# A gather of rows by index: other places for the distinct indices, own loads for the first two batches, four direct batches instead of five

## The chip, the cores and the metric

The kernel runs on one core of a Trainium2 chip. The metric is the device time of one execution in microseconds (us), as the median over several runs. The profile also gives a span, from the first to the last recorded event; it is about 2 us shorter than the device time. A run on a single core is called slow here when it took over 1.5% more than the fastest run of the same kernel; comparisons use the fast runs alone.

## The reference

```python
x       = randn(32, 512, 1024)        # float32
indices = randint(0, 512, (32, 128))  # the same draw in every run
for b in range(32):
    result[b] = x[b, indices[b]]      # 128 rows of 4096 bytes
```

Some indices of a batch repeat: the draw has 109 to 120 distinct ones among the 128 of each batch.

## The kernel before

The first five batches (`HEAD`) are "direct": all 128 rows are gathered and written out. For each of the other 27 batches the kernel works out the distinct indices and gathers each distinct row only once. The remaining places, 8 to 18 in these batches, get an index out of bounds, and nothing is moved for them. A matmul with a matrix of zeros and ones then spreads the rows to their final places. These batches gather into a ring of eight buffers, which are zeroed first so that skipped places hold no leftovers.

```python
HEAD, RING, FAR = 5, 8, 1024
...
idx0 = const.tile([N, 1], indices.dtype, name="idx0")       # the indices of batch 0 by themselves
nc.sync.dma_start(out=idx0[:], in_=indices.rearrange("b n -> n b")[:, 0:1])
...
for b in range(HEAD):                                       # the direct batches
    gather(blocks[b], idx0[:].bitcast(I32)[:, 0:1] if b == 0 else idxT[:, b:b + 1], b)
    nc.sync.dma_start(out=of[b * N:(b + 1) * N], in_=blocks[b][:])
...
def prep(g0, g1):                                           # the "index step" of a group of batches
    ...                                                     # lead: first of its kind; slot: its rank
    for b in range(g0, g1):
        first = (79 * b) % N
        pack = junkp.tile([N, N], F16, name="pack")
        turned = turn[:].rearrange("p t n -> p (t n)")[:, N - first:2 * N - first]
        nc.vector.tensor_scalar(out=pack[:], in0=turned, scalar1=slot[:, b:b + 1],
                                scalar2=lead[:, b:b + 1], op0=ALU.is_equal, op1=ALU.mult)
        nc.tensor.matmul(sm[:, 1, b - g0:b - g0 + 1], lhsT=pack[:], rhs=near[:, b:b + 1], ...)
    nc.vector.tensor_scalar(out=at[:, w], in0=sm[:, 1, :n], ...)   # at: the indices to gather
...
for k in range(RING):                                       # eight zeroed buffers
    if k < 3:
        nc.vector.memset(u[:], 0.0)
    else:
        nc.scalar.copy(out=u[:], in_=held[0][:])            # five copies that read buffer 0
...
groups = [(HEAD, HEAD + 3)] + [(g, min(g + 4, B)) for g in range(HEAD + 3, B, 4)]
for b in range(HEAD, B):
    ...                                                     # prep of a later group
    u = held[(b - HEAD) % RING]
    gather(u, at[:, b:b + 1], b, bounds_check=S - 1, oob_is_err=False)
    ...                                                     # matmul, two copies out, write
```

The row `turned` says which place of the buffer each rank gets. Before, rank s of batch b goes to place (s + 79b) mod 128: the skipped places are one stretch, which moves on from batch to batch.

## Time and profile before

| | before |
|---|---|
| time, median of the first three runs | 89.34 us (88.88 to 89.35) |
| span of the profiled run | 87.1 us |
| moved | 32.12 MB |
| rate from 17 us to the last slice but two | about 418 GB/s |
| last packet of each of the 16 DMA engines | 82.5 to 85.5 us |

The prediction below shows the strips of this page and reads them. The busy time by stretches at the end (start and end, length, then busy us with counts for PE, its weight loads, DVE, ACT and POOL, then the clock, the DMA share and GB/s):

```profile
75.00:81.00 6.00, 3.85 (x8) 1.35 (x8) 1.75 (x3) 1.76 (x3) 0.00 (x0) 1.00 1.03 420
81.00:87.10 6.10, 0.00 (x0) 0.00 (x0) 0.00 (x0) 0.00 (x0) 0.00 (x0) 0.59 0.52 214
```

The rate stays at 420 GB/s to 81 us, when PE has been done for a while. The timeline near 20 us (start, duration, engine, line, operation, and in brackets the idle time before and what ended it):

```profile
17.40 0.99 POOL L79 DMA_INDIRECT u<-in_x_dram,at  x1 [0.30 <-issue]
20.34 0.35 PE L119 MATMUL sm<-near,pack 128*128 128x1 f16 x3 [4.06 <-DVE pack L117]
20.55 2.06 PE L148 MATMUL ps<-u,s 128*128 128x512 f32 x2
22.65 0.16 DVE L121 TENSOR_SCALAR at<-sm 128x4 int32<-128x4 f32 x1 [1.41 <-PE sm L119]
23.08 0.99 POOL L79 DMA_INDIRECT u<-in_x_dram,at  x1 [4.70 <-DVE atF L122]
```

Twelve gathers have been issued by 18.4 us. The thirteenth is the first of the third group and waits for that group's indices (`at`), which come at 22.65.

### The profile page before, as it was taken

To read this page: it belongs to the slowest core of one execution; us is meant where nothing else is said; L and a number is where in the kernel's file an instruction comes from. 1 tells how busy PE (TensorE), PEld (TensorE's weight loads), DVE (VectorE), ACT (ScalarE), POOL (GpSimd) and SP (SyncE) were. 2 spreads that over 40 slices of the span, in tenths; PEclk is the share of its full clock that TensorE was granted. 3 is DMA by queue.
4 is the path that set the end of the run, shared out by engine and by line. 5 is a ranking of instruction groups with operands and counts; after the bars stand their busy time and mean duration, and the time that the engine had idled before them with its cause. 6 is when DMAs were issued, how large, how long until landed. Compare 5 with 4: busy or idle time off the path is not lost.

```text
span 87.1 us, 784 instructions
## 1 busy us (share of the span) xinstructions
PE 58.0 (67%) x169; PEld 23.9 (27%) x169; DVE 47.3 (54%) x181; ACT 21.9 (25%) x33; POOL 32.3 (37%) x38
## 2 busy tenths in 40 slices
PE   0043502006999999999999999877978877793000
PEld 0031301003434444433443443222322333230000
DVE  4989994107539979587997357833141133333000
ACT  0997000000022222342322234031222222223000
POOL 3577787740354464618545461663200000000000
PEclk9999999999999999999999999999999999999855
DMA  0178999999999999999999999999999999999960
GB/s 4 27 207 224 322 373 363 416 421 418 418 420 420 416 421 418 420 416 421 418 421 410 416 420 427 406 420 420 418 420 418 420 420 414 421 420 420 414 256 15
DMA packets 9603, 32.12 MB, mean 369 GB/s; under 512 B 1751, under 2 KB 1783, under 8 KB 9600
## 3 DMA queue, kind: packets, MB, share of 16 engines
q1 hardware_dynamic: 4848, 16.80, 47.3%
q0 software_dynamic: 4608, 15.24, 45.5%
q10 hardware_dynamic: 144, 0.05, 0.2%
q8 instruction: 1, 0.02, 0.1%
q14 instruction: 2, 0.02, 0.0%
HBM read 16.84 MB, written 16.78 MB: 386 GB/s over the span
## 4 chain that ended last, share of the span: by engine, by line
DMA 35%; DVE 19%; issue 13%; PE 12%; POOL 7%; another core or an unknown queue 3%; ACT 1%; POOLq 1%; DVEq 0%
DMA u<-in_x_dram,at 35%; PE ps L148 11%; POOL u L79 7%; DVE junk L105 6%; DVE pack L117 4%; DVE u L133 2%; DVE block L150 2%; DVE s L125 2%; ACT block L151 1%; POOLq L79 1%; PE bc L101 1%; DVE slot L112 0%; DVE lead L108 0%; PE sm L119 0%
## 5 line engine op out<-in xcount | busy, mean ns | idle before, releaser
L148 PE MATMUL ps<-u,s 128*128 128x512 f32 x108 | 53.2, 629 | 4.5 <-DMA u<-in_x_dram,at 4.2
L79 POOL DMA_INDIRECT u<-in_x_dram,at x27 | 26.7, 990 | 25.5 <-DVE atF L122 9.1
L150 DVE COPY block<-ps 128x512 f32<-128x512 f32 x27 | 18.6, 691 | 22.9 <-PE ps L148 19.1
L151 ACT COPY block<-ps 128x512 f32<-128x512 f32 x27 | 15.8, 586 | 56.3 <-DVE block L150 54.1
L148 PEld LDWEIGHTS ps<-u,s 128*128 128x128 f32 x108 | 19.0, 196 | 29.4 <-issue 27.2
L105 DVE SCALAR_TENSOR_TENSOR junk<-bc,idxF,below 128x128 f16<-128x128 f32 x27 | 8.8, 345 | 0.9 <-issue 0.5
L117 DVE TENSOR_SCALAR pack<-turn,slot,lead 128x128 f16<-128x128 int32 x27 | 7.6, 358 | 2.9 <-remote 2.8
L101 PE MATMUL bc<-vf,ident 32*128 32x128 f16 x27 | 3.3, 263 | 7.7 <-DVE ident L67 5.0
L125 DVE TENSOR_SCALAR s<-bc,atF 128x128 f32<-128x128 f32 x27 | 7.6, 345 | 0.1
L119 PE MATMUL sm<-near,pack 128*128 128x1 f16 x27 | 3.4, 174 | 5.2 <-DVE pack L117 5.0
L119 PEld LDWEIGHTS <-pack 128*128 128x128 f16 x27 | 2.5, 102 | 11.4 <-DVE pack L117 8.2
L101 PEld LDWEIGHTS <-ident 32*128 32x128 f16 x27 | 2.1, 113 | 9.8 <-DVE ident L67 5.0
L135 ACT COPY u<-u 128x1024 f32<-128x1024 f32 x5 | 4.8, 1041 | 0.0
L79 POOL DMA_INDIRECT block<-in_x_dram,idxT x4 | 3.8, 941 | 1.5 <-issue 0.9
L111 PE MATMUL sm<-lead,above 128*128 128x4 f16 (+1 forms) x7 | 1.2, 170 | 3.7 <-DVE junk L105 2.3
L133 DVE MEMSET u<- 128x1024 f32 x3 | 2.7, 912 | 1.3 <-PEq L167 1.0
L121 DVE TENSOR_SCALAR at<-sm 128x4 int32<-128x4 f32 (+1 forms) x7 | 1.1, 162 | 2.5 <-PE sm L119 2.3
L105 DVE DVE_READ_ACCUMULATOR junk<-bc,idxF,below 128x1 f32 x27 | 2.3, 84 | 0.0
L135 ACT ACT_TABLE_LOAD x1 | 1.3, 1283 | 2.1 <-issue 2.1
L111 PEld LDWEIGHTS <-above 128*128 128x128 f16 x7 | 0.7, 103 | 3.7 <-DVE junk L105 2.6
L112 DVE COPY slot<-sm 128x4 f32<-128x4 f32 (+1 forms) x7 | 1.1, 155 | 1.2 <-issue 1.2
L79 POOL DMA_INDIRECT block<-in_x_dram,idx x1 | 1.1, 1098 | 1.6 <-DMA idx<-in_indices_dram 1.6
(17 smaller groups left out, 5.9 us busy)
## 6 DMA issues: line engine op xcount, KB each, us to landing
out_dram<-block SPq DMA_DIRECT2D x32, 512.0 KB, 8.9
u<-in_x_dram,at POOLq DMA_INDIRECT x27
block<-in_x_dram,idxT POOLq DMA_INDIRECT x4
v<-in_indices_dram ACTq DMA_DIRECT2D x2, 8.0 KB
v<-in_indices_dram SPq DMA_DIRECT2D x2, 8.0 KB, 1.8
v<-in_indices_dram ACTq DMA_DIRECT2D x1, 32.0 KB
idx<-in_indices_dram SPq DMA_DIRECT2D x1, 1.0 KB
block<-in_x_dram,idx POOLq DMA_INDIRECT x1
```

The lines of the kernel that those rows point to most:

```text
L79: nc.gpsimd.indirect_dma_start(out=dst[:], out_offset=None, in_=xf[:], in_offset=bass.IndirectOffsetOnAxis(ap=at, axis=0), element_offset= ...
L101: nc.tensor.matmul(bc[:, b - g0], lhsT=ident[:B, b:b + 1].to_broadcast([B, N]), rhs=vf[:], start=True, stop=True)
L105: nc.vector.scalar_tensor_tensor(out=junk[:], in0=bc[:, b - g0], scalar=idxF[:, b:b + 1], in1=below[:], op0=ALU.is_equal, op1=ALU.mult, ac ...
L111: nc.tensor.matmul(sm[:, 0, :n], lhsT=above[:], rhs=lead16[:, w], start=True, stop=True)
L117: nc.vector.tensor_scalar(out=pack[:], in0=turned, scalar1=slot[:, b:b + 1], scalar2=lead[:, b:b + 1], op0=ALU.is_equal, op1=ALU.mult)
L119: nc.tensor.matmul(sm[:, 1, b - g0:b - g0 + 1], lhsT=pack[:], rhs=near[:, b:b + 1], start=True, stop=True)
L125: nc.vector.tensor_scalar(out=s[:], in0=bc[:, b - g0], scalar1=atF[:, b:b + 1], scalar2=None, op0=ALU.is_equal)
L133: nc.vector.memset(u[:], 0.0)
L135: nc.scalar.copy(out=u[:], in_=held[0][:])
L148: nc.tensor.matmul(ps[:, h * 512:(h + 1) * 512], lhsT=spread[b][:], rhs=u[:, h * 512:(h + 1) * 512], start=True, stop=True)
L150: nc.vector.tensor_copy(out=blocks[b][:, :512], in_=ps[:, :512])
L151: nc.scalar.copy(out=blocks[b][:, 512:], in_=ps[:, 512:])
```

## The change

It has three parts. The distinct indices are dealt in turn to sixteen groups of eight neighbouring partitions, so that the skipped places spread evenly over what it takes for the 16 DMA engines. The indices of batches 0 and 1 get a small load each, so that the second gather need not wait for the transposed table. And there are four direct batches instead of five, with a first group of two batches; only two buffers are then zeroed by DVE and six by ACT.

```diff
-    HEAD, RING, FAR = 5, 8, 1024
+    HEAD, RING, FAR = 4, 8, 1024
...
-    idx0 = const.tile([N, 1], indices.dtype, name="idx0")
-    nc.sync.dma_start(out=idx0[:], in_=indices.rearrange("b n -> n b")[:, 0:1])
+    first = []
+    for b, eng in ((0, nc.sync), (1, nc.scalar)):
+        t = const.tile([N, 1], indices.dtype, name=f"first{b}")
+        eng.dma_start(out=t[:], in_=indices.rearrange("b n -> n b")[:, b:b + 1])
+        first.append(t[:].bitcast(I32)[:, 0:1])
...
-    turn = const.tile([N, 2, N], I32, name="turn")
-    nc.gpsimd.iota(turn[:], pattern=[[0, 2], [1, N]], base=0, channel_multiplier=0)
...
+    turn = const.tile([N, 2, 16, N // 16], I32, name="turn")
     for b in range(HEAD):
-        gather(blocks[b], idx0[:].bitcast(I32)[:, 0:1] if b == 0 else idxT[:, b:b + 1], b)
+        if b == 2:
+            nc.gpsimd.iota(turn[:], pattern=[[0, 2], [1, 16], [16, N // 16]], base=0, channel_multiplier=0)
+        gather(blocks[b], first[b] if b < 2 else idxT[:, b:b + 1], b)
...
-            first = (79 * b) % N
+            at0 = (3 * b) % 16 * (N // 16)
-            turned = turn[:].rearrange("p t n -> p (t n)")[:, N - first:2 * N - first]
+            turned = turn[:].rearrange("p t e j -> p (t e j)")[:, at0:at0 + N]
...
-        if k < 3:
+        if k < 2:
             nc.vector.memset(u[:], 0.0)
...
-    groups = [(HEAD, HEAD + 3)] + [(g, min(g + 4, B)) for g in range(HEAD + 3, B, 4)]
+    groups = [(HEAD, HEAD + 2)] + [(g, min(g + 4, B)) for g in range(HEAD + 2, B, 4)]
```

## The prediction

> **What bounds the kernel now.** I read the page first (the strips in 40 slices, the DMA queues, the chain), then the busy time by stretches, then the timeline of the gathers and of the matmuls, and last the packet records of the trace themselves. The page, cut:
>
> ```profile
> span 87.1 us, 784 instructions
> ...
> PE   0043502006999999999999999877978877793000
> ...
> DMA  0178999999999999999999999999999999999960
> GB/s 4 27 207 224 322 373 363 416 421 418 418 420 420 416 421 418 420 416 421 418 421 410 416 420 427 406 420 420 418 420 418 420 420 414 421 420 420 414 256 15
> DMA packets 9603, 32.12 MB, mean 369 GB/s; under 512 B 1751, under 2 KB 1783, under 8 KB 9600
> ...
> q1 hardware_dynamic: 4848, 16.80, 47.3%
> q0 software_dynamic: 4608, 15.24, 45.5%
> ```
>
> A slice is 2.18 us. From slice 8 to slice 38 the transfers run at some 418 GB/s with all 16 DMA engines busy; only the first seven slices and the last two are not full. q0 holds the gathers, q1 the writes. The busy time by stretches (columns: PE, weight loads, DVE, ACT, POOL, clock, DMA share, GB/s) says the same of every stage after 10 us:
>
> ```profile
> 5.00:10.00 5.00, 2.02 (x15) 1.44 (x16) 4.62 (x31) 3.24 (x4) 3.78 (x5) 1.00 0.90 267
> 10.00:20.00 10.00, 1.78 (x13) 1.00 (x10) 4.97 (x29) 0.00 (x0) 6.56 (x7) 1.00 1.00 385
> 20.00:56.00 36.00, 34.95 (x105) 14.87 (x106) 26.71 (x104) 9.38 (x16) 16.82 (x17) 1.00 1.03 418
> 56.00:75.00 19.00, 15.39 (x32) 5.20 (x31) 5.64 (x9) 4.69 (x8) 2.98 (x3) 1.00 1.03 419
> ```
>
> PE is full from 20 to 56 us but is only working off what has landed; then it catches up and waits for each gather, every 2.5 us (timeline, PE: start, duration, wait):
>
> ```profile
> 65.19 1.96 PE L148 MATMUL ps<-u,s 128*128 128x512 f32 x4 [0.55 <-DMA u<-in_x_dram,at]
> 67.69 1.95 PE L148 MATMUL ps<-u,s 128*128 128x512 f32 x4 [0.54 <-DMA u<-in_x_dram,at]
> 70.20 1.96 PE L148 MATMUL ps<-u,s 128*128 128x512 f32 x4 [0.56 <-DMA u<-in_x_dram,at]
> ```
>
> So the DMA engines bound it. The packet records refine this. They hold queue, start, duration and size. A 4096-byte row takes 159 ns and is followed on its engine by the next one after some 155.5 ns; a 4-byte record (a skipped row, or the closing count of a transfer) takes 6. With these two steps I linked the records after 20 us into sequences, one for each engine. They show no idle time on any engine from 20 us to its last packet. **An engine's end is therefore its start plus its own number of rows by 155.5 ns.** The last packets end between 82.5 and 85.5 us: the slowest single engine sets the time, not the mean.
>
> **What the Trainium skill says, and whether the trace agrees.**
> 1. "DMA: Bandwidth & Descriptors", section "The descriptor swizzle": of 128 partitions an engine gets four and the four that lie 32 further on, engine = 8*(p>>6) + ((p>>2)&7); not eight neighbours. The change deals to eight neighbours, so I tested it. From the drawn indices (109 to 120 distinct in a batch) I wrote down for each engine the order of moved and skipped rows in the old placement. Eight of the linked sequences, of 224 to 231 marks each, agree with the skill's map without one miss (engines 0, 1, 3, 5, 8, 9, 12, 15); under a map of eight neighbours the same sequences miss at least 17 marks each. The expected 375 skipped rows are there too: 4608 records less 512 closings less 3721 rows. The trace agrees with the page, for this indirect gather as well.
> 2. Same page, "Queues, rings and completion order": an engine takes turns between queues with work. Agrees: gathered and written rows alternate in the sequences. Eight gathered and eight written rows and two closings are 16 x 0.1555 + 0.01 = 2.50 us, the matmuls' rhythm.
> 3. Same page, "Why a DMA increments its semaphore by 16 and not by 1": a transfer has landed only when all its engines have. So the engine with the most rows sets each gather's landing.
>
> **The change, part by part.**
> *Dealing.* Slot s now goes to place e = s mod 16, j = s div 16 of partition 8e+j, turned by a multiple of 8. Empty slots (s from 109..120 up to 127) have j = 7, seldom 6. Such a partition lies in the upper four of its eight, so p>>2 is odd, whatever the turn: by the skill's map **all skipped rows fall to the odd engines and none to the even ones**. Counted from the indices, rows of both queues for each engine: before 481 to 496 (mean 489); after 512 on the eight even engines and 461 to 465 on the odd. The even ones now read as if nothing were skipped. Against the mean engine that is +23 rows x 0.1555 = +3.6 us; against the largest of before +16 rows = +2.5 us.
> *The slow head.* At 20 us the nine sequences I can name had moved 70 to 88 rows (mean 80) of the 98 that fit into the time since the first gather at 4.8 us. Engine 3 had 75 done and 493 in all: 20.1 + 418 x 0.1555 + 0.35 (small packets) = 85.5, the end seen. After the change the slowest of eight even engines should have about 73 done by 20 us: 20.05 + 439 x 0.1555 + 0.45 = 88.8 us. That is +3.3 us.
> *Own index load of batch 1.* The gathers were issued so:
>
> ```profile
> 3.00 1.10 POOL L79 DMA_INDIRECT block<-in_x_dram,idx  x1 [1.63 <-DMA idx<-in_indices_dram]
> 4.63 0.94 POOL L79 DMA_INDIRECT block<-in_x_dram,idxT  x1 [0.54 <-DVE idxF L63]
> 5.88 0.94 POOL L79 DMA_INDIRECT block<-in_x_dram,idxT  x1 [0.31 <-issue]
> ...
> 9.62 1.00 POOL L79 DMA_INDIRECT u<-in_x_dram,at  x1 [0.30 <-issue]
> ```
>
> The second no longer waits 0.54 us but the usual 0.30: at 4.40, 0.23 us earlier, and it is queued before the first has drained, which saves part of the slow first packets of a restarted queue: my estimate is 0.3 to 0.4 us in all. The second iota (0.34 us) moves behind it and delays the third gather and those after it by about 0.15 us.
> *Two memsets, six copies.* DVE has one memset less (0.91 us), ACT one copy more (1.04 us). The first ring gather overwrites the buffer that those copies read, and waits for them. They took this long:
>
> ```profile
> 3.41 4.83 ACT L135 COPY u<-u 128x1024 f32<-128x1024 f32 x5
> ```
>
> Six of them, starting some 0.4 us later behind one more index load on that queue, end at about 3.85 + 5.8 = 9.7 us; with four direct batches that gather would otherwise go at 8.5. So gathers from the fifth on go some 1.2 us later than the fifth did. The queue then still holds rows, so I count 0 to 0.3 us: this and the earlier second gather about cancel.
> *One direct batch less.* 13 rows fewer to read in all, all on odd engines: nothing. PE gets a 28th batch, 1.96 us, in a stage where it catches up anyway: nothing.
> *Sum:* end of the last packet 88.8 instead of 85.5. From last packet to measured time are 89.34 - 85.5 = 3.84 us, unchanged: 92.6. I put it at 92.5.
>
> **Rivals.**
> (a) *The intended effect.* If engines served eight neighbours, the largest load would fall from 497 to 489 rows, -1.25 us, and with the head 87.8 us. For it speaks only the intent; the exact match of the sequences speaks against it.
> (b) *Even out by luck.* If the slow start falls on odd engines this time, the even ones have some 80 rows done at 20 us: end 87.7, time 91.5, near the 2% line of 91.1.
> (c) *The chain after the last gather.* The even engines alternate 1:1, so their last gathered row comes late, near 83.6 us by 20.05 + (204 + 204) x 0.1557. After it come the matmul, the two copies, the issue (3.8 us in the old end) and the last write (1.25 us, some 0.5 to start): 89.2, time 93.0. It ends about where the load does; whichever is later counts.
> (d) *A dry queue near 24 us.* Only ten gathers instead of twelve precede the third group's indices, which the semaphores gave late (22.65 us) before. 80 + 32 rows last the even engines until about 24.6 us. If the eleventh gather comes later than 23 us, they run dry, up to 1.5 us.
>
> **Range and chances.** (b) gives the lower edge, (c) and (d) together the upper: 91.2 to 93.9. Faster needs (a): 0.03. Within 2% needs luck as in (b) and no dry queue: 0.11. Slower by over 2%: 0.86.
>
> **What would show it.** Right: records linked as above give eight engines with 512 rows and eight with 461 to 465; the odd ones fall idle in between, so GB/s drops below 418 through the middle and the late slices, to about 400 (512 + 463 over 2 x 512 of full rate is 95%); PE waits for gathers earlier than 56 us, at 2.5 us per batch to the end; the first ring gather on POOL waits for ACT until about 9.7 us. Wrong: a rate still at 418 to 420 GB/s until the last two slices with all engines ending together, which would mean the placement or the map is not what I counted; or a hole in the DMA strip near slice 11, which would mean (d).

## The result and the profile after

The changed kernel took **93.05 us** (median of 4 runs, 92.90 to 93.95, all fast) against 89.13 us for the kernel before. The ratio is 1.046, with a 95% interval of 1.038 to 1.054: slower. Here and below a ratio is the mean time of one kernel's fast runs over that of the other's of the same rounds, so it is not quite the ratio of the medians quoted. Differences of medians below are good to about half a microsecond.

The page of the changed kernel:

```profile
span 91.4 us, 813 instructions
...
PE   0032520399999999999977777557777777888000
...
DMA  0189999999988999999999999999999998777760
GB/s 4 32 256 285 346 375 386 393 420 405 377 258 328 418 416 420 418 418 418 423 413 416 423 409 420 411 420 421 416 418 418 420 411 330 319 305 308 303 253 9
...
q1 hardware_dynamic: 4848, 16.80, 45.3%
q0 software_dynamic: 4608, 15.18, 43.7%
```

The bytes are practically the same, yet the strips show two places that were full before. **A hole** near slice 11 (258 and 328 GB/s, at 25 to 30 us), and **a late fall** from slice 33 on (about 310 GB/s, from 75 us). The busy time by stretches, with the columns as above:

```profile
20.00:56.00 36.00, 33.32 (x102) 13.10 (x100) 26.31 (x106) 9.37 (x16) 17.85 (x18) 1.00 1.00 399
56.00:75.00 19.00, 13.71 (x30) 4.94 (x30) 5.65 (x12) 4.09 (x7) 3.96 (x4) 1.00 1.02 417
75.00:81.00 6.00, 4.73 (x10) 1.84 (x11) 1.80 (x3) 1.76 (x3) 0.00 (x0) 1.00 0.82 334
81.00:87.00 6.00, 3.09 (x7) 0.87 (x5) 1.38 (x2) 1.17 (x2) 0.00 (x0) 1.00 0.74 300
```

Between the hole and 75 us the rate is 417 GB/s, no less than before. From 75 us it falls to 334, where the kernel before still had 420 to 81 us, and then to 300. PE still has batches to do up to 87 us.

The packet records tell what the engines do meanwhile. I summed the time that rows occupy in each microsecond, at 0.156 us a row. In the hole, from 22 to 30 us, this gives 15.0, 14.1, 14.9, 11.3, 10.6, 8.7, 12.3 and 14.3 engines' worth of work out of 16: 26.8 engine-microseconds lost, or 1.7 us for each engine. Not all of it is idle time. In the hole 49 rows took over 200 ns, up to 891 ns, where a row takes 159 ns otherwise; these slow rows are some 11 of the 26.8. (That is why the DMA strip shows 8 and 9 there and the rate shows the hole better.) The kernel before has no such row from 22 to 30 us. In the late fall the work is that of 8 to 10 engines in five of the twelve microseconds from 76 to 88 us, and more in the others, where more written rows come along. The kernel before has all 16 busy from 16 to 81 us. Its last gathered row ends at 76.4 us; the changed kernel's at 82.0. Another count is the rows started per engine, as the mean of 16:

| rows started per engine by | 20 us | 30 us | 75 us | in all |
|---|---|---|---|---|
| before | 79.8 | 143.5 | 430.2 | 488.6 |
| after | 82.1 | 135.2 | 421.4 | 487.5 |

The head is 2 rows ahead, the hole costs some 10 rows (about 1.6 us at 0.1555 us a row), and nothing is lost or won from 30 to 75 us. Then comes the uneven end.

In the head, the lines that the prediction spoke of (timeline):

```profile
3.90 5.78 ACT L140 COPY u<-u 128x1024 f32<-128x1024 f32 x6
4.17 0.95 POOL L80 DMA_INDIRECT block<-in_x_dram,first  x1 [0.30 <-issue]
10.18 1.00 POOL L80 DMA_INDIRECT u<-in_x_dram,at  x1 [2.15 <-DVE pack L122]
```

The second gather starts at 4.17 after the usual 0.30 us. The six zeroing copies end at 9.68, and the first ring gather follows at 10.18 after 2.15 us of idling. The indices (`at`) were ready at 9.39 already. So I take it that the gather waited for the copies; the releaser named is a DVE step that happened to come last in the records.

And the hole, in the timelines of the engines:

```profile
16.72 0.99 POOL L80 DMA_INDIRECT u<-in_x_dram,at  x1 [0.30 <-issue]
17.52 2.08 PE L153 MATMUL ps<-u,s 128*128 128x512 f32 x2 [3.46 <-DMA u<-in_x_dram,at]
19.39 0.27 PE L124 MATMUL sm<-near,pack 128*128 128x1 f16 x3
21.29 0.69 DVE L155 COPY block<-ps 128x512 f32<-128x512 f32 x1 [5.19 <-PE sm L124]
21.90 0.15 DVE L126 TENSOR_SCALAR at<-sm 128x4 int32<-128x4 f32 x1
22.32 0.98 POOL L80 DMA_INDIRECT u<-in_x_dram,at  x1 [4.61 <-DVE atF L127]
```

Ten gathers are out by 17.7 us. The eleventh needs the third group's indices. In PE's order the first matmul of the first ring batch, which waits for its gather's landing (3.46 us), stands ahead of that group's small matmuls (`sm<-near,pack`); on DVE the copy of that batch stands ahead of `at`. So the indices come at 21.90 and the eleventh gather at 22.32. The thirteenth came at 23.08 before: about as late, but with two more batches queued ahead of it.

The end, in PE's timeline:

```profile
80.18 1.95 PE L153 MATMUL ps<-u,s 128*128 128x512 f32 x4 [0.54 <-DMA u<-in_x_dram,at]
82.68 1.52 PE L153 MATMUL ps<-u,s 128*128 128x512 f32 x3 [0.55 <-DMA u<-in_x_dram,at]
```

PE waits for each gather to the end, 2.50 us apart: the time of 8 gathered and 8 written rows on one engine. (The fourth record of the last batch begins after this view's window.) In e1 below, which deals by the true engines, PE waits for gathers 2.36 to 2.38 us apart from 53 to 60 us. The last landing is at 82.55 us by the chain of waits, and then follow the matmul, two copies and the last write. The engines have their last packets from 88.1 to 88.4 us, and a single straggler at 90.0.

### The profile page after: what moved, and what is told of

It reads as the page before. It is cut to its first block, busy times and chain, and to the rows that moved or that the text cites. A ratio compares the mean times of both kernels' runs of the same rounds, so it can differ in the third digit from the quotient of the medians.

```text
span 91.4 us, 813 instructions
## 1 busy us (share of the span) xinstructions
PE 60.7 (66%) x176; PEld 24.2 (27%) x176; DVE 48.6 (53%) x190; ACT 23.4 (26%) x35; POOL 32.7 (36%) x38
## 4 chain that ended last, share of the span: by engine, by line
DMA 50%; PE 24%; DVE 10%; issue 7%; ACTq 1%; ACT 1%; POOLq 0%; POOL 0%; DVEq 0%
DMA u<-in_x_dram,at 48%; PE ps L153 22%; DVE junk L110 3%; DVE block L155 2%; DMA v<-in_indices_dram 2%; DVE pack L122 2%; PE bc L106 1%; DVE near L74 1%; ACT block L156 1%; DVE below L72 1%; PE sm L124 1%; ACTq L47 1%; ACTq L43 0%; POOL u L80 0%; DVE lead L113 0%
## 5 line engine op out<-in xcount | busy, mean ns | idle before, releaser
L153 PE MATMUL ps<-u,s 128*128 128x512 f32 x112 | 55.9, 628 | 13.3 <-DMA u<-in_x_dram,at 13.1
L80 POOL DMA_INDIRECT u<-in_x_dram,at x28 | 27.8, 993 | 30.2 <-PE ps L153 10.6
L155 DVE COPY block<-ps 128x512 f32<-128x512 f32 x28 | 19.3, 688 | 33.0 <-PE ps L153 24.2
L156 ACT COPY block<-ps 128x512 f32<-128x512 f32 x28 | 16.4, 585 | 59.9 <-DVE block L155 59.9
L140 ACT COPY u<-u 128x1024 f32<-128x1024 f32 x6 | 5.8, 1040 | 0.0
L124 PE MATMUL sm<-near,pack 128*128 128x1 f16 x28 | 2.7, 171 | 1.0 <-DVE pack L122 0.8
L80 POOL DMA_INDIRECT block<-in_x_dram,first x2 | 2.0, 1018 | 2.0 <-DMA first<-in_indices_dram 1.7
L138 DVE MEMSET u<- 128x1024 f32 x2 | 1.8, 912 | 1.2 <-PEq L172 1.0
L80 POOL DMA_INDIRECT block<-in_x_dram,idxT x2 | 1.9, 940 | 0.5 <-issue 0.3
L113 DVE TENSOR_SCALAR lead<-cnt 128x4 f16<-128x4 f32 (+1 forms) x8 | 1.4, 175 | 0.1
```

Of the source, the lines that this page charges most:

```text
L80: nc.gpsimd.indirect_dma_start(out=dst[:], out_offset=None, in_=xf[:], in_offset=bass.IndirectOffsetOnAxis(ap=at, axis=0), element_offset= ...
L153: nc.tensor.matmul(ps[:, h * 512:(h + 1) * 512], lhsT=spread[b][:], rhs=u[:, h * 512:(h + 1) * 512], start=True, stop=True)
L155: nc.vector.tensor_copy(out=blocks[b][:, :512], in_=ps[:, :512])
L156: nc.scalar.copy(out=blocks[b][:, 512:], in_=ps[:, 512:])
```

## The experiments

Twelve kernels ran. All gave correct results. The kernel before took 89.24 to 89.34 us. The theory: dealing over eight neighbours loads the even engines (the late fall), and ten gathers ahead are too few (the hole). The rivals: one of the two carries everything, or dealing is harmless and something in the head costs.

| kernel | what differs | median us (range) | before in the same rounds | ratio (95%) |
|---|---|---|---|---|
| e1_map_in_after | after, dealt over the true engines | 90.60 (90.20–90.84) | 89.24 | 1.013 (1.004–1.022) |
| e2_map_in_before | before, dealt over the true engines | 89.07 (88.77–89.74) | 89.24 | 0.995 (0.986–1.003) |
| e3_deal8_in_before | before, the change's dealing alone | 91.93 (91.38–93.45) | 89.24 | 1.025 (1.016–1.033) |
| e4_old_place_in_after | after without the dealing | 91.07 (90.70–92.24) | 89.24 | 1.016 (1.005–1.026) |
| e5_group4_in_after | after, first group of four | 92.11 (91.62–92.30) | 89.30 | 1.029 (1.024–1.035) |
| e6_map_group4_in_after | e1 with first group of four | 89.38 (88.61–89.86) | 89.30 | 1.002 (0.997–1.008) |
| e7_own_loads_in_before | before, own loads alone | 88.65 (88.39–88.96) | 89.30 | 0.993 (0.988–0.999) |
| e8_group1_in_before | before, first group of one | 89.53 (89.27–90.57) | 89.30 | 1.005 (0.996–1.013) |
| e9_map_own_loads | e2 with own loads | 88.27 (87.79–89.25) | 89.34 | 0.990 (0.984–0.996) |
| e10_half_deal8 | half the batches dealt over eights | 90.64 (90.39–90.91) | 89.34 | 1.015 (1.009–1.021) |
| e11_head5_in_e6 | e6 with five direct batches | 88.39 (88.23–88.60) | 89.33 | 0.986 (0.979–0.993) |
| e12_head5_in_after | after with five direct batches | 91.65 (91.42–92.71) | 89.33 | 1.022 (1.014–1.029) |

The medians are over all runs of a kernel. e3, e4 and e9 have one slow run each; so have the runs of before beside e1 to e4 and beside e11 and e12, and three of the eleven beside e9 and e10 are slow. The fast runs alone give 91.78 for e3, 90.96 for e4 and 89.10 for before beside e3 and e4, so the differences stay the same. Where it matters I use these.

### The dealing alone, added and taken away (e3, e4)

e3 puts only the changed dealing into the kernel before; e4 puts only the old places back into the changed kernel.

```diff
# e3, in the kernel before
-    turn = const.tile([N, 2, N], I32, name="turn")
-    nc.gpsimd.iota(turn[:], pattern=[[0, 2], [1, N]], base=0, channel_multiplier=0)
+    turn = const.tile([N, 2, 16, N // 16], I32, name="turn")
+    nc.gpsimd.iota(turn[:], pattern=[[0, 2], [1, 16], [16, N // 16]], base=0, channel_multiplier=0)
-            first = (79 * b) % N
+            at0 = (3 * b) % 16 * (N // 16)
-            turned = turn[:].rearrange("p t n -> p (t n)")[:, N - first:2 * N - first]
+            turned = turn[:].rearrange("p t e j -> p (t e j)")[:, at0:at0 + N]
# e4: the same lines the other way round, in the changed kernel
```

> The kernel before, with only the changed kernel's dealing over groups of eight partitions. Loads 512 and 463 to 467. Theory: this one part costs nearly all: 19 rows more on the slowest engine are 3.0 us, 91.8 to 92.8 us. Rival: if the uneven load is hidden by the eight gathers in flight, it stays at 89 to 90 us.

> The changed kernel with the old placement put back: index loads, four direct batches, groups and memsets as changed. Theory: 89.0 to 90.2 us, what the rest of the change costs alone, with the hole in the transfers near 22 to 29 us still there if it comes from the indices of the third group arriving late. Rival (the dry queue is a consequence of the dealing): at or under 89.0 us, and no hole.

e3 took 91.93 us, 2.7 us more than before by the medians (2.2 by the ratio). Its profiled run was the slow one (93.45 us), so I take only the shape from its strips:

```profile
DMA  0088999999999999999999999999999987777730
GB/s 6 23 233 249 295 349 363 424 414 422 419 417 415 421 417 406 426 415 419 415 406 419 419 419 419 419 419 419 421 419 415 422 353 326 324 315 310 301 136 7
```

The late fall is there (326 to 301 GB/s), and there is no hole. The dealing alone makes the late fall, and it does not make the hole.

e4 took 91.07 us, 1.8 us more than before (1.4 by the ratio). That is more than I expected: I had put the rest of the change at no more than about 1 us. Its rate in 40 slices:

```profile
GB/s 1 29 233 297 332 381 387 401 387 418 330 269 235 370 405 425 418 416 423 405 416 414 423 418 412 422 416 420 416 423 420 414 418 420 420 418 422 422 231 18
```

And its eleventh gather in POOL's timeline:

```profile
23.26 0.99 POOL L80 DMA_INDIRECT u<-in_x_dram,at  x1 [5.45 <-DVE atF L127]
```

Here is the hole without the late fall. The two costs, 2.7 and 1.8 us, add up to 4.5 against 3.9 for the whole change. That the whole is a little less may be because part of the hole falls on odd engines, which have time to spare; it is also within the error of such differences.

### Dealing over the engines that the records show (e1, e2)

Both use the same edit. The ranks go in turn to the 16 engines by the map that the prediction tested, engine = 8*(p>>6) + ((p>>2)&7), instead of to eight neighbours.

```diff
+            by = (3 * b) % 16
+            turned = turn[:].rearrange("p t n -> p (t n)")[:, by:by + N]
+            nc.vector.tensor_scalar(out=pack[:].rearrange("p (a m r) -> p a m r", a=2, m=16),
+                                    in0=turned.rearrange("p (r m a) -> p a m r", r=4, m=16),
+                                    scalar1=slot[:, b:b + 1],
```

> The changed kernel, with the distinct indices dealt in turn to the engines as the packet records of before show them (four partitions and the four that lie 32 further on), nothing else. Rows for each engine become 486 to 489 instead of 512 and 461 to 465. Theory (the uneven load sets the end): the end comes 24 x 0.1555 = 3.7 us earlier less what a slow head leaves, so 89.0 to 90.3 us. Rival (the rest of the change, above all the dry queue and the later ring gathers, costs most of the 4 us): it stays over 91.5 us.

> The kernel before, with only the placement changed to the deal over the engines that the records show. Largest load 490 instead of 496. Theory: the ends, which now spread from 82.5 to 85.5 us, can only narrow by the part that comes from the rows (some 1 us); the slow head keeps its part. 88.0 to 88.9 us. Rival (even loads in each batch also make each gather land sooner and keep PE fed, so that more is won): under 87.5 us.

e1 took 90.60 us, 2.45 less than the changed kernel's 93.05: what the dealing had cost is gone, and the hole is still there (the eleventh gather at 23.04 after 5.40 us of idling):

```profile
GB/s 1 30 248 257 294 357 399 411 422 422 374 277 226 392 411 420 420 420 416 420 418 414 420 416 405 424 418 418 418 418 416 422 420 416 422 420 414 427 322 13
```

It is a little above the expected range; the likely reason is that the hole costs more than I had put down.

e2 took 89.07 us; its interval includes no change at all. So the intended effect, all engines equally loaded (487 to 490 rows by the indices), is worth at most a little in the kernel before, less than I expected. In the profiled run one engine had its last packet at 86.25 us and all others by 85.1. The kernel before was already within 8 rows of even, and a single late engine takes back what the rows give.

### A half dose (e10)

Odd batches are dealt over eights, even batches over the true engines, in the kernel before.

```diff
+            if b % 2:
+                dealt = eights[:].rearrange("p t e j -> p (t e j)")[:, by * (N // 16):by * (N // 16) + N]
+                ...                     # the changed dealing
+            else:
+                ...                     # as in e2
```

> A half dose: the kernel before, with odd batches dealt over eights and even batches over the engines that the records show. The even engines get 498 to 502 rows, the odd ones 474 to 480. Theory (time follows the largest number of rows on one engine): half way between the two full doses, 89.1 us at 490 rows and 91.9 at 512, so 90.3 to 90.9 us. Rival (the cost comes from something else in dealing over eights, or uneven batches are evened out while eight gathers are in flight): at either end, under 89.6 or over 91.5 us.

It took 90.64 us. With the largest load of an engine worked out from the indices, three kernels that differ in nothing but the places (e10 also builds a second table for them) line up: 490 rows, 89.07 us (e2); 502 rows, 90.64 us (e10); 512 rows, 91.78 us (e3, fast runs). That is 2.7 us for 22 rows, or 0.12 us a row; a row takes 0.1555 us on its engine. So the time follows the largest load, as the prediction's step from rows to time said, at about 80% of a row's time for each row more.

### More gathers ahead of the third index step (e5, e6)

A first group of four instead of two gives twelve gathers ahead, in the changed kernel (e5) and with the true engines (e6).

```diff
-    groups = [(HEAD, HEAD + 2)] + [(g, min(g + 4, B)) for g in range(HEAD + 2, B, 4)]
+    groups = [(g, min(g + 4, B)) for g in range(HEAD, B, 4)]
```

> The changed kernel, with four batches instead of two in the first group of indices, so that twelve gathers instead of ten are issued before the third group's indices are needed. The dealing over eights stays. Theory (the hole at 22 to 29 us comes from too few gathers ahead of late indices, and the even engines lose some of it too): the hole is gone, the uneven end stays; 91.6 to 92.5 us, like the dealing alone in the kernel before (91.9). Rival (the hole falls on odd engines only, which have time to spare): unchanged, 92.8 to 93.3 us, hole or no hole.

> The changed kernel with both mended: dealt over the engines that the records show, and a first group of four. Theory (two independent costs): the 90.6 us of the first mend less the 1.5 to 2.3 us of the hole; 88.3 to 89.1 us, level with the kernel before or a little under it. Rival (the later ring gathers, which wait for the longer zeroing copies, cost by themselves): 89.6 us or more with no hole left.

e5 gained 0.9 us (92.11 against 93.05) and e6 gained 1.2 us (89.38 against 90.60). In e5 the hole was not gone but smaller and spread out. In e6 all engines are busy from about 17 us on. But with a larger first group the index step of that group is longer, and the first ring gather starts at 10.82 instead of 10.18; the thin stretch moves to 8 to 17 us. e6 came out between its theory and its rival, about as fast as the kernel before.

### Ten gathers ahead in the kernel before (e8)

A first group of one makes it ten gathers ahead of the third group, as in the changed kernel.

```diff
-    groups = [(HEAD, HEAD + 3)] + [(g, min(g + 4, B)) for g in range(HEAD + 3, B, 4)]
+    groups = [(HEAD, HEAD + 1)] + [(g, min(g + 4, B)) for g in range(HEAD + 1, B, 4)]
```

> The kernel before with a first group of one batch instead of three, so that only ten gathers stand before the third group's indices, as in the changed kernel; but here the built order puts that group's index step ahead of the first matmul of a gathered batch and of the first copy out, where the changed kernel has them behind. Theory (late because of the place in the engines' order, behind a gather's landing): indices early, no hole, 89.0 to 89.6 us. Rival (ten ahead are too few in any order, or the semaphores stall as before until 22 us): a hole near 24 us and 90.3 us or more.

It took 89.53 us, and there is no hole. The timeline says why:

```profile
17.45 0.21 PE L119 MATMUL sm<-near,pack 128*128 128x1 f16 x2 [0.50 <-DVE junk L105]
18.13 0.99 POOL L79 DMA_INDIRECT u<-in_x_dram,at  x1 [2.30 <-DVE atF L122]
20.34 3.78 PE L148 MATMUL ps<-u,s 128*128 128x512 f32 x4 [2.68 <-DMA u<-in_x_dram,at]
```

In this kernel the scheduler placed the third group's small matmuls ahead of the first ring matmul. The indices do not wait for any gather's landing, and the eleventh gather starts at 18.13. So ten gathers ahead are not too few by themselves. The runs together (table below) say that it takes both: few gathers ahead, and the index step behind the first landing. No run moves the index step ahead in the changed kernel with its four direct batches, so for that kernel itself this is argued from e8 and e12.

### Own index loads alone, and with the true engines (e7, e9)

```diff
-    idx0 = ...
+    own = []
+    for b, eng in ((0, nc.sync), (1, nc.scalar)):
+        t = const.tile([N, 1], indices.dtype, name=f"own{b}")
+        eng.dma_start(out=t[:], in_=indices.rearrange("b n -> n b")[:, b:b + 1])
+        own.append(t[:].bitcast(I32)[:, 0:1])
-        gather(blocks[b], idx0[:].bitcast(I32)[:, 0:1] if b == 0 else idxT[:, b:b + 1], b)
+        gather(blocks[b], own[b] if b < 2 else idxT[:, b:b + 1], b)
```

> The kernel before with one part alone: the indices of batches 0 and 1 loaded by themselves on two queues. Theory: the second gather goes some 0.3 to 0.5 us earlier and the first at about 2.8 us; the queue is fuller from 5 to 8 us; worth 0.2 to 0.5 us: 88.6 to 89.1 us, a difference that three rounds may not resolve. Rival (more small packets and a later load of the other indices take it back): 89.2 to 89.6 us.

> The kernel before with the two parts that paid or did no harm: the indices of batches 0 and 1 loaded by themselves, and the deal over the engines that the records show. Five direct batches and the old groups stay. Theory: the own loads' 0.65 us, and from the even rows 0 to 0.4 us more: 88.2 to 88.8 us, faster than before by under 1%. Rival (the two gains overlap, or the strided write of the placement matrix costs on DVE): 89 us or more.

e7 took 88.65 us, 0.65 less than before. The gain is small, but its interval does not include zero. Its mechanism is not shown: by 20 us the engines of its profiled run had started 80.2 rows on average against 79.8, which is 0.06 us, and over all kernels here this count varies between 77 and 82. e9, with five rounds, took 88.27 us, 1.0% less than the kernel before (0.4 to 1.6%). It is faster than both kernels, though by less than 2%.

### Five direct batches put back (e11, e12)

```diff
-    HEAD, RING, FAR = 4, 8, 1024
+    HEAD, RING, FAR = 5, 8, 1024
```

e11 does this in e6, e12 in the changed kernel with nothing else touched.

> The changed kernel with the even dealing and a first group of four took 89.38 us, and the best kernel so far, which differs from it in one direct batch more, a first group of three and the order of a few steps, 88.27. Theory: the difference of about 1.1 us comes from the first ring gather, which with four direct batches is the fifth gather and waits for its zeroed buffer until about 10.2 us, where with five it is the sixth and the waiting is partly filled by a fifth direct gather; the thin stretch at 8 to 19 us shrinks. With five direct batches it takes 88.2 to 88.8 us. Rival: the fifth direct batch is worth nothing, the difference lies in the group of four (its index step is longer and comes later): 89.2 or more.

> The changed kernel (93.05 us) with five direct batches in place of four and nothing else changed: eleven gathers ahead of the third index step in place of ten, the dealing over eights stays. Theory: the hole at 22 to 30 us, about 1.7 us per engine, is gone or small, and the uneven end, worth about 2.7 us alone, stays: 91.5 to 92.5 us. Rival: the number of direct batches does not matter to the hole, since the third group's index step still stands behind the first ring batch's copies out: 92.7 to 93.3 us.

e12 took 91.65 us, 1.4 less than the changed kernel (both against their own runs of before: 1.022 and 1.046). The hole is gone: all 16 engines are busy from 18 us to 72 us but for a few tenths, and 141.7 rows are started per engine by 30 us against 135.2. What is left is the late fall, and the time is about that of the dealing alone (e3):

```profile
GB/s 3 27 258 281 341 274 353 405 425 411 425 413 423 414 420 413 418 418 422 409 420 413 425 411 423 413 420 416 420 418 418 418 377 342 326 305 310 299 198 9
```

The timeline shows more than I had expected:

```profile
15.85 0.16 DVE L126 TENSOR_SCALAR at<-sm 128x4 int32<-128x4 f32 x1
20.39 5.93 PE L153 MATMUL ps<-u,s 128*128 128x512 f32 x7 [4.57 <-DMA u<-in_x_dram,at]
24.44 0.99 POOL L80 DMA_INDIRECT u<-in_x_dram,at  x1 [4.13 <-PE ps L153]
```

As in e8, the third group's indices are now ahead of the first ring matmul, at 15.85. Thirteen gathers are out when POOL stops, and it then waits for a ring buffer (`ps`), not for indices. So e12 confirms that the fifth direct batch is what the hole lacked; it does not say how much of it is the longer queue and how much the order, since both came with it.

e11 took 88.39 us, 1.0 less than e6 and as much as e9 (88.27). So the fifth direct batch was also what separated e6 from e9; the rival, that the group of four did it, is out. Its first ring gather still starts at 10.80, as in e6, but it is now the sixth gather and not the fifth: a direct one fills part of the time before it. It also has one more gather ahead of the third step. I did not separate these two.

### The hole in all kernels

| kernel | gathers ahead of the third group's | its indices in PE's order | hole |
|---|---|---|---|
| after, e1, e4 | 10 | behind the first ring matmul | yes, at 22 to 30 us |
| e5, e6 | 12 | behind | e5: several dips; e6: none after 17 us |
| before, e3 | 12 | partly ahead, partly behind | no |
| e11 | 13 | behind | no |
| e8 | 10 | ahead | no |
| e12 | 11 | ahead | no |

e2, e7, e9 and e10 keep the groups of the kernel before, and none of them has a hole.

## Why the prediction was right

The range held: 92.5 us was said, 93.05 came. The main mechanism, the uneven load, was right. That the number came so close is partly luck: the dealing was put at 3.3 us and measured 2.7, the own loads gave more than was said, and a cost put at nothing, the missing direct batch, measured 1.4 us. By its own steps:

- **The map and the dealing: right.** e3 and e10 show that the dealing over eight neighbours costs time by itself, by 0.12 us for each row more on the fullest engine, and e1 shows that dealing by the map takes it back. Predicted for the dealing was +2.5 to +3.6 us, or +3.3 with the slow head; measured 2.7 (e3, medians). The counts of 512 and 461 to 465 rows are from the indices; the records of the changed kernel agree with them. Linked back from the end, a late engine shows eight rows in each gather, none skipped, and no gap back to 27 us (ending at 88.3); no odd engine's order of rows fits it. Two details were off. A 4-byte record lasts 9 ns in the records; 6 ns is the step to the next one. And 8 to 19 skipped rows is the range over all 32 batches; it is 8 to 18 over those that skip.
- **Where the rate falls: wrong.** I expected about 400 GB/s through the middle, with odd engines idle in between. It was 417 from 56 to 75 us and fell only then. Up to eight gathers can be under way at once, as the ring has eight buffers; the likely reason, not tested, is that odd engines run ahead with the gathers already queued, so their free time gathers at the end. An estimate from the counts fits: an even engine that ends at 88.3 without a gap has some 85 rows left at 75 us; the mean engine has 66, so an odd one has about 47 of its 463 left. In proportion that is some two batches ahead of the even engines.
- **PE's waits: right.** PE waits for gathers from 43.8 us on (said: earlier than 56; in the kernel before from 55.8), for most of the time 2.50 us apart.
- **The head: right in its parts.** The second gather went after the usual 0.30 us (4.17), the six copies ended at 9.68 (said: 9.7), the first ring gather came at 10.18. The own loads give 0.65 us (e7), where I estimated 0.3 to 0.4.
- **"One direct batch less … nothing", and the ring gathers' delay that "about cancels" the earlier second gather: the step that failed.** The bytes are indeed nothing, and so is PE's extra batch. But the fifth direct batch was the last work in the queue that needs no index step. Without it the rest of the change costs 1.8 us (e4), and putting it back into the changed kernel gives 1.4 us (e12). I had counted a batch's rows and not what it keeps the queue busy through.
- **Rival (d), the dry queue: came true.** Up to 1.5 us was said; 1.7 us per engine was lost on average. It said the wait for the eleventh gather would have to pass 23 us; the gather came at 22.32 already, and the engines began to run dry at 22. (Its 24.6 us for the end of the 112 queued rows does not follow from the 73 rows at 20 us that it uses elsewhere, which give 26.1; the mean of 80 gives 25.0.) I did not see that the order on PE and DVE has a part in it (e8, e12), since I took the late indices of the kernel before as given.
- **Rival (c), the chain after the last gather: right in form.** The last landing was at 82.55 (said: 83.6). From there to 88.2, about where most engines end, are 5.65 us; I said 89.2 − 83.6 = 5.6. Most even engines had their load done at about the same time, so I cannot tell which of the two set their end.
- **The slowest even engine: later than said.** It was to end at 88.8. Linked back from its end, the straggler at 90.0 fits an even engine and no odd one, so it is the one to compare: 1.2 us later. It shows no gap back to 59 us, so it was already some 10 rows behind the others there (1.6 us at 0.1555 us a row). How much of this comes from the head and how much from the hole is open.
- **Rival (a): out.** Even by the true map, the intended effect is worth 0.2 us in the kernel before, with an interval that includes zero (e2), not the 1.25 that (a) set down.
- **Rival (b): open in part.** It put the even engines at some 80 rows by 20 us in place of 73. The mean of all engines was 82.1, but I did not count the even ones by themselves. The dealing alone cost 2.7 us (e3), between the 2.2 of (b) and the 3.3 of the main line.
- **From the last packet to the time.** I subtracted a profiled packet end (85.5) from a median of other runs (89.34). The profiled run itself took 89.03, so the tail is 3.5 us and not 3.84. In the changed kernel it is 93.18 − 90.01 = 3.2 us. So this term was over by 0.3 to 0.7 us, and hid part of what the hole and the straggler added: in the profiled run the last packet was 1.2 us later than said and the tail 0.7 us shorter, which leaves 93.2 against 92.6.

The sum by measured parts, in medians: 89.3 before, +2.7 (dealing, e3), −0.65 (own loads, e7), +1.4 (four direct batches, e12 against after) make 92.75; measured 93.05. The parts do not add up in every order: e4, the rest of the change under the old places, costs 1.8 us, where −0.65 and +1.4 make only 0.75.

## What to carry to other kernels

These come from this one kernel. Before spreading work "evenly over the DMA engines", read from the packet records which partitions an engine serves, and count rows per engine from real data: an even deal over the wrong groups is worse than a rough one, and the fullest engine sets the time. Work that needs no preparation, such as a direct gather, is worth more than its bytes at the start, because it keeps the queue full until the first prepared work is ready. When indices come late, look at the order of the instructions on the engines that make them: a step that stands behind another's wait for a landing inherits that wait.

## What the Trainium skill lacked or had wrong

- "DMA: Bandwidth & Descriptors", section "Specifications", gives "Partitions per engine: 8 (convention)" and does not say which eight. The section "The descriptor swizzle" has it right, and it holds for an indirect gather with skipped rows as well: eight linked sequences without one miss. The cost of taking them for neighbours was 2.7 us of 89.2 (e3).
- No page says what a row skipped for its index costs on its engine. In the records it is a 4-byte packet after which the engine's next one starts 6 ns later, against 155.5 ns for a row of 4096 bytes, so skipped rows shorten only the engine that they fall to.
- Same page, section "Queues, rings and completion order", has an engine drain a whole packet of typically 9 to 17 descriptors from one queue before it turns to the next. In the kernel before, from 30 to 70 us, 1433 of the 1669 runs of gathered rows in the linked sequences were a single row before a written row came: the turns are row by row here.
- Same page, section "Latency and other measured facts", has engines 7 and 15 usually slower. No run here showed that: the last engine to end was another in each of the kernels that I could name it in (3 before, 10 in e2, 1 in e1; in the changed kernel, e3 and e12 one with an even number). In five of the profiled runs one engine ended 1.1 to 1.8 us after all others (90.0 against 88.4 in the changed kernel); this is on no page, and no run explains it. In three of them (e2, e3, e12) the profiled run was the slowest of its kernel.
- No page says that rows are slow where the queue of gathers has just started or run dry: in the kernel before, from 4.8 to 14 us, 103 gathered rows took over 200 ns and up to 1.16 us instead of 159 ns, about 2.1 us in sum for each engine; in the hole of the changed kernel 49 rows did. Why is not shown.
